# Dealing eight SBUF slots in fixed rotation to loads and outgoing images of a Winograd-style convolution

## The chip, the cores and the metric

The kernel runs on one core of one Trainium2 chip. The metric is the time of one execution in microseconds of the device, the median of several runs. A run's *span*, from its first instruction to the end of its work, is about 1.8 us shorter than its time. Some executions are slower than the others of the same kernel; a run counts as *slow* when it is over 1.5% above the fastest run of the same kernel, and else as *fast*.

## The reference

```python
batch, c_in, h, w, c_out = 16, 64, 64, 64, 128      # x: fp32; weight: 128 x 64 x 3 x 3, fp32
x_pad = pad(x, one pixel of zeros around each image)
output[b, co] += weight[co, ci, kh, kw] * x_pad[b, ci, kh:kh+h, kw:kw+w]     # all b, co, ci, kh, kw
```

It is a 3x3 convolution. The input is 16.8 MB of fp32, the output 33.5 MB of fp32.

## The kernel before

Two images form a *pair*, so that 2 x 64 input channels fill 128 partitions; there are eight pairs. The kernel combines rows so that two output rows share one product (`G1` with row sums `ss`). TensorE makes the products in PSUM (the memory that it accumulates in), ScalarE (ACT) copies the shared one to `ut`, and VectorE (DVE) adds that to each of the others, which writes the output images `ot`. GpSimd (POOL) makes the row sums.

Memory is what this study is about: SBUF, the core's on-chip memory of 128 partitions. One fp32 pair (`xf`) takes 16 KB of each partition, and so does one outgoing image (`ot`); a pair has two of these. All come from one pool of eight 16 KB slots:

```python
big = ctx.enter_context(tc.tile_pool(name="big", bufs=8))
NH = 5
cuts = [(0, 18), (18, 34), (34, 50), (50, 64)]

def load(p):                                   # pairs 0 to 4: fp32, cast to fp16 by ScalarE later
    xf[p] = big.tile([128, H, W], F32, tag="big", name="xf")
    for lo, hi in cuts if p == 0 else [(0, H)]:
        keep(nc.sync.dma_start(xf[p][:, lo:hi, :], x_rows[128*p : 128*p+128, lo:hi, :]))

def outs(p):                                   # the two outgoing images of a pair
    ots[p] = [big.tile([128, H // 2, 2, W], F32, tag="big", name="ot") for _ in range(2)]

def load_cast(p):                              # pairs 5 to 7: the DMA casts to fp16, other memory
    xs[p] = xpool.tile([128, H, W], F16, tag="xc", name="xc")
    keep(nc.gpsimd.dma_start(xs[p], x_rows[128*p : 128*p+128, :, :]))

for p in range(NH): load(p)
outs(0)
# ... weights ...
for p in range(NP):                            # NP = 8
    if p not in ots: outs(p)
    # POOL: row sums of pair p+1; at p == 0 also load_cast(5..7)
    for blk in range(4):
        U = group([(G1, None)]);  us = [scalar.copy(U[b2]) for b2 in 0, 1]
        # ScalarE: some casts xf -> xs of coming pairs
        A = group([(G21, 1), (G0, -1)])
        # VectorE: ot row 0 of each row pair = A + us   (L184)
        Bt = group([(G01, 0), (G2, 2)])
        # VectorE: ot row 1 = Bt + us                   (L187)
        parts = {3: (0, 64)} if p < NP - 1 else {1: (0, 32), 3: (32, 64)}
        if blk in parts:                       # 2 MB per image; the last pair in two halves
            lo, hi = parts[blk]
            for b2 in range(2):
                keep(nc.sync.dma_start(out_rows[2*p + b2, :, lo:hi, :], ots[p][b2] ...))   # L192
```

A new tile in a used slot has to wait until the slot's last user is done: for a load, that its casts and row sums were made; for an outgoing image, that its store has landed. With `bufs=8` and one tag, the framework chooses the slot. The waits in the program as built tell its choice: pair 2's first image got load 1's slot, and its *second image got the slot of store 0's first image*. Pairs 3 to 5 are mixed in the same way: one image in a load's slot, the other in that of an earlier store.

## Time and profile before

| | before |
|---|---|
| time, median of 3 (range) | 133.56 us (133.37 to 134.36) |
| span of the profiled run | 132.2 us |
| TensorE busy | 108.4 us (82%) |
| longest wait of VectorE | 9.1 us, for an outgoing DMA |
| arithmetic ends / last store lands | 122.6 us / 131.0 us |

The profile's page cuts the span into 40 slices of 3.3 us; a digit is the busy share in tenths, and `PEclk` is the granted TensorE clock:

```profile
span 132.2 us, 2428 instructions
...
PE   0389999999992059999999999999999999997000
...
PEclk9999999999999757999999999999999999999965
DMA  4999999999999999999999999699469937999992
GB/s 138 304 376 451 416 451 402 352 315 310 327 310 327 315 322 330 404 441 412 451 416 421 441 412 426 288 397 471 169 273 441 397 164 317 456 414 394 434 436 89
```

TensorE has one hole, near 40 to 48 us. DMA is full until then and long after, and has holes, stretches in which the engines run out of transfers, only after 82 us (6, 4, 6, 3, 7). The list of waits (engine and tile, what it waited for, total us, times, longest) names the hole:

```profile
DVE ot L184 <- DMA out_dram<-ot: 9.1, 1, 9.1
PE acc L164 <- DVE ot L184: 7.3, 1, 7.3
```

One event, told twice: VectorE waits once for 9.1 us, and TensorE, whose PSUM tiles are not emptied meanwhile, stands still for 7.3 us. The timeline of VectorE shows where (start, length, engine, line, what; in brackets the idle time before it and what ended it):

```profile
37.20 0.69 DVE L184 TENSOR_TENSOR ot<-acc,ut 128x512 f32<-128x512 f32 x1 [0.72 <-PE acc L164]
46.99 0.69 DVE L184 TENSOR_TENSOR ot<-acc,ut 128x512 f32<-128x512 f32 x1 [9.10 <-DMA out_dram<-ot]
```

These are the first adds of pair 2's two images. The second starts at 46.99 us, just after store 0's first image landed (46.86 us, issued at 23.10: it stood in line behind loads that were still coming). The chain of waits, followed back from the last instruction, runs through that store:

```profile
PE 63%; DMA 22%; DVE 3%; ACT 2%; issue 1%; DVEq 1%; SPq 0%
PE acc L164 63%; DMA out_dram<-ot 18%; DMA xf<-in_x_dram 4%; DVE ot L184 2%; ACT xs L62 1%; DVE ot L187 1%; DVE ss L89 1%; DVEq L221 0%; ACT ut L178 0%; SPq L45 0%; DVEq L184 0%
```

By stretches (length, busy time of each engine, granted clock, mean share of the 16 DMA engines that was busy, where 1 or a little over is full, GB/s), TensorE is the limit late in the kernel, with DMA not far behind:

```profile
core 0: us, PE busy (x) PEld busy (x) DVE busy (x) ACT busy (x) POOL busy (x), PEclk, DMA share, GB/s
45.00:51.00 6.00, 3.27 (x16) 1.35 (x17) 4.00 (x7) 0.00 (x0) 0.00 (x0) 0.50 1.04 328
84.00:96.00 12.00, 12.00 (x116) 6.10 (x114) 9.21 (x16) 3.81 (x8) 0.82 (x1) 1.00 0.83 351
96.00:108.00 12.00, 12.00 (x116) 6.08 (x112) 9.21 (x16) 4.29 (x8) 0.00 (x0) 1.00 0.83 351
```

The first of these lines shows an echo of the hole: after the standstill the granted clock was 0.50. The Trainium skill, "TensorE: Matmul & The Clock Gate", section "What's actually happening", says that an idle TensorE falls to half its clock after some 3.4 us and is released by activity; this trace agrees (idle from 40.4 us, half clock from 44.6 to 51.4 us).

### The profile page before, as it was taken

What the parts mean: (1) busy time and instruction counts of PE and PEld (TensorE: products, weight loads), DVE (VectorE), ACT (ScalarE), POOL (GpSimd) and SP (SyncE); (2) the same over time, 40 slices, a digit from 0 to 9 for tenths busy, and PEclk for the clock granted to TensorE, in tenths of its full rate; (3) what the DMA queues carried; (4) which work ended last, traced back from release to release, by engine and by line L of the source; (5) the groups of instructions that cost most, each with busy time, mean ns of one, the idle gap of its engine ahead of it and who ended that gap; (6) DMA issues with size and microseconds to landing.
All of it is one profiled execution on the core that took longest, in us unless ns stands there. A gap on an engine that the chain in (4) does not pass through costs nothing.

```text
span 132.2 us, 2428 instructions
## 1 busy us (share of the span) xinstructions
PE 108.4 (82%) x978; PEld 55.3 (42%) x978; DVE 84.1 (64%) x135; ACT 55.9 (42%) x88; POOL 33.8 (26%) x23
## 2 busy tenths in 40 slices
PE   0389999999992059999999999999999999997000
PEld 0335455555550024455545455545554555443000
DVE  0278857877720075787777877877787778777000
ACT  3283878969694004843333333333333333332000
POOL 2000399967076000390047006600000000000000
PEclk9999999999999757999999999999999999999965
DMA  4999999999999999999999999699469937999992
GB/s 138 304 376 451 416 451 402 352 315 310 327 310 327 315 322 330 404 441 412 451 416 421 441 412 426 288 397 471 169 273 441 397 164 317 456 414 394 434 436 89
DMA packets 4330, 47.62 MB, mean 360 GB/s; under 512 B 480, under 2 KB 480, under 8 KB 1120
## 3 DMA queue, kind: packets, MB, share of 16 engines
q1 hardware_dynamic: 3888, 44.34, 80.4%
q0 software_dynamic: 432, 3.15, 11.4%
q8 instruction: 7, 0.11, 0.3%
q14 instruction: 3, 0.02, 0.0%
HBM read 17.07 MB, written 33.55 MB: 383 GB/s over the span
## 4 chain that ended last, share of the span: by engine, by line
PE 63%; DMA 22%; DVE 3%; ACT 2%; issue 1%; DVEq 1%; SPq 0%
PE acc L164 63%; DMA out_dram<-ot 18%; DMA xf<-in_x_dram 4%; DVE ot L184 2%; ACT xs L62 1%; DVE ot L187 1%; DVE ss L89 1%; DVEq L221 0%; ACT ut L178 0%; SPq L45 0%; DVEq L184 0%
## 5 line engine op out<-in xcount | busy, mean ns | idle before, releaser
L164 PEld LDWEIGHTS <-Wt 64*128 64x128 f16 x960 | 54.1, 96 | 61.6 <-issue 13.5
L164 PE MATMUL acc<-xs,Wt 64*128 64x504 f16 (+3 forms) x480 | 63.2, 385 | 7.4 <-DVE ot L184 7.3
L184 DVE TENSOR_TENSOR ot<-acc,ut 128x512 f32<-128x512 f32 x64 | 41.3, 685 | 31.4 <-PE acc L164 19.9
L178 ACT COPY ut<-acc 128x512 f32<-128x512 f32 x64 | 34.4, 590 | 59.0 <-issue 44.1
L187 DVE TENSOR_TENSOR ot<-acc,ut 128x512 f32<-128x512 f32 x64 | 41.1, 684 | 0.0
L164 PE MATMUL acc<-ss,Wt 64*128 64x504 f16 (+1 forms) x192 | 36.1, 392 | 1.5 <-DVE ss L89 1.5
L164 PE MATMUL acc<-xc,Wt 64*128 64x504 f16 (+3 forms) x288 | 35.0, 373 | 0.0
L89 POOL TENSOR_TENSOR ss<-xf 128x1024 f16<-128x1024 f32 x8 | 18.8, 2369 | 20.1 <-DMA xf<-in_x_dram 14.0
L62 ACT CAST xs<-xf 128x1024 f16<-128x1024 f32 (+2 forms) x20 | 20.4, 1058 | 0.9 <-DMA xf<-in_x_dram 0.9
L89 POOL TENSOR_TENSOR ss<-xc 128x1024 f16<-128x1024 f16 x6 | 12.6, 2128 | 30.3 <-issue 30.3
L89 DVE TENSOR_TENSOR ss<-xf 128x512 f16<-128x512 f32 x4 | 2.8, 689 | 3.4 <-DMA xf<-in_x_dram 3.4
L107 PE MATMUL wp<-ident,w 128*64 128x128 f16 x18 | 1.3, 328 | 4.1 <-DVE w L79 4.1
L107 PEld LDWEIGHTS <-w 128*64 128x64 f16 x18 | 1.1, 210 | 4.1 <-DVE w L79 4.1
L79 DVE CAST w<-w_raw 128x576 f16<-128x576 f32 x1 | 0.5, 460 | 3.6 <-DMA w_raw<-in_weight_dram 3.6
L71 POOL DMA_DIRECT2D xc<-in_x_dram x3 | 1.8, 599 | 0.0
L109 ACT CAST Wt<-wp 128x384 f16<-128x384 f32 x1 | 0.5, 479 | 2.8 <-PE wp L107 2.8
L109 ACT ACT_TABLE_LOAD x1 | 1.3, 1283 | 0.7 <-PEq L210 0.7
L114 ACT CAST Wt<-wp 128x384 f16<-128x384 f32 x1 | 0.5, 479 | 0.5 <-DVE Wt L112 0.5
L111 DVE TENSOR_TENSOR Wt<-wp,Wt 128x384 f16<-128x384 f32 x1 | 0.5, 549 | 0.0
L112 DVE TENSOR_TENSOR Wt<-wp,Wt 128x384 f16<-128x384 f32 x1 | 0.5, 546 | 0.0
L115 ACT CAST Wt<-wp 128x384 f16<-128x384 f32 x1 | 0.5, 484 | 0.0
masks.py:199 POOL TENSOR_SCALAR_AFFINE_SELECT ident<-ident 128x128 f16<-128x128 f16 x1 | 0.3, 294 | 0.1
(5 smaller groups left out, 0.6 us busy)
## 6 DMA issues: line engine op xcount, KB each, us to landing
out_dram<-ot SPq DMA_DIRECT2D x14, 2048.0 KB, 11.8
xf<-in_x_dram SPq DMA_DIRECT2D x4, 2048.0 KB, 19.7
out_dram<-ot SPq DMA_DIRECT2D x4, 1024.0 KB, 8.3
xc<-in_x_dram POOLq DMA_DIRECT2D x3, 1024.0 KB, 24.4
xf<-in_x_dram SPq DMA_DIRECT2D x2, 512.0 KB, 6.2
xf<-in_x_dram SPq DMA_DIRECT2D x1, 576.0 KB, 5.0
xf<-in_x_dram SPq DMA_DIRECT2D x1, 448.0 KB, 7.8
w_raw<-in_weight_dram SPq DMA_DIRECT2D x1, 288.0 KB, 2.9
```

Source lines behind the costliest of these rows:

```text
L62: keep(nc.scalar.copy(xs[p][:, lo:hi, :], xf[p][:, lo:hi, :]))
L71: keep(nc.gpsimd.dma_start(xs[p], x_rows[128 * p : 128 * p + 128, :, :]))
L79: keep(nc.vector.tensor_copy(w16, w_raw))
L89: eng.tensor_add(ss[p][:, lo : lo + n, :], v[:, lo : lo + n, 0, :], v[:, lo : lo + n, 1, :])
L107: nc.tensor.matmul(wp[q : q + 64, k * CO : k * CO + CO], w16[:, t::9], ident)
L109: keep(nc.scalar.copy(wrow(G1), wps[1]))
L111: keep(nc.vector.tensor_sub(wrow(G21), wps[2], wrow(G1)))
L112: keep(nc.vector.tensor_sub(wrow(G01), wps[0], wrow(G1)))
L164: nc.tensor.matmul(tiles[b2][:, lo - j0 : hi - j0, c_lo:c_hi], Wt[p0 : p0 + 64, wi, kw, :], rhs, start=i == 0, stop=i == n - 1,)
L178: keep(nc.scalar.copy(ut, U[b2]))
L184: nc.vector.tensor_add(ots[p][b2][:, j0 : j0 + RB, 0, :], A[b2], us[b2])
L187: nc.vector.tensor_add(ots[p][b2][:, j0 : j0 + RB, 1, :], Bt[b2], us[b2])
```

## The change

The intent is that a tile takes the slot whose last user began longest ago, so that no outgoing image waits for a store that was only just issued. Eight tags with one buffer each fix the choice by hand:

```diff
-    big = ctx.enter_context(tc.tile_pool(name="big", bufs=8))
+    big = ctx.enter_context(tc.tile_pool(name="big", bufs=1))
 ...
+    slot = [0]
+
+    def next_slot(shape, name):
+        slot[0] += 1
+        return big.tile(shape, F32, tag=f"slot{(slot[0] - 1) % 8}", name=name)
 ...
-        xf[p] = big.tile([128, H, W], F32, tag="big", name="xf")
+        xf[p] = next_slot([128, H, W], "xf")
 ...
-        ots[p] = [big.tile([128, H // 2, 2, W], F32, tag="big", name="ot") for _ in range(2)]
+        ots[p] = [next_slot([128, H // 2, 2, W], "ot") for _ in range(2)]
```

Loads 0 to 4 take slots 0 to 4, pair 0 takes 5 and 6, pair 1 takes 7 and 0, pair 2 takes 1 and 2 (loads 1 and 2), pair 3 takes 3 and 4, and from pair 4 on each pair takes the slots of the pair four before it. No instruction and no size changes.

## The prediction

> **What bounds the kernel now.** The span is 132.2 us (median run 133.56). The list of waits shows two long ones of one event: the vector engine's first add of an image pair waits 9.1 us for an outgoing DMA, and the tensor engine 7.3 us for that add. In the timeline it is pair 2: its first such add ends its wait at 46.99, when pair 0's first store (issued 23.10) landed. The chain of waits runs through that store (18%), then 72 us of unbroken matmuls; from 48 to 120 us TensorE is busy throughout. The second limit is close: DMA is busy 92% of the span, without a hole to about 82 us, at some 428 GB/s; later holes sum to 7.5 us (its packets, in 3 us stretches).
>
> **What the change does.** No instruction, size or order changes; only addresses, and so waits. In the program as built before, pair 2's images took load 1's slot and that of *store 0's first image*; pairs 3 to 5 mix likewise. With rotation, pair 2 takes loads 1 and 2, pair 3 loads 3 and 4, pair 4 pair 0's slots, 5 pair 1's, 6 pair 2's, 7 pair 3's.
>
> **Costed.**
> - Pair 2's second image needs load 2's casts (ended 31.3) and Pool sums (26.4), against its turn near 37.9: no wait. The 9.1 us goes; pair 3 starts near 50.0, not 59.16 (pairs start 12.8 us apart).
> - Pair 3 needs load 4's casts (expected near 47.5) and Pool sums (41.9): little or no wait.
> - Pair 4, near 62.8, needs store 0 (landed 55.5); pair 5, near 75.6, store 1 (65.25); pairs 6 and 7, at 88 and 101, stores 2 and 3 (about 75 and 85): no wait.
> - So arithmetic ends near 113.4, not 122.6: 9.1 us earlier.
> - The stores cannot follow. After store 1 lands at 65.25, ten 2 MB stores at 4.85 us (their landings in the full stretch) and four of 1 MB at 2.43 us remain: 65.25 + 48.5 + 9.7 = 123.5 us. A pair's stores are issued every 12.8 us and take 9.7, so the backlog shrinks but just does not empty before the end. Last landing 123.5, not 131.0: 7.5 us gained, the same as the sum of the holes.
>
> The Trainium skill, "DMA: Bandwidth & Descriptors", section "Where 436 GB/s comes from", gives 435 GB/s as the ceiling at the SBUF ports; this trace's 428 agrees, so I expect no faster stores.
>
> **On the critical path:** 7.5 of the 9.1 us. The end turns from compute-bound to store-bound.
>
> **Predicted: 126.1 us, 8 in 10 within 125.0 to 127.8.** Faster by over 2%: 0.96; within 2%: 0.035; slower: 0.005.
>
> **What the profile would show.** Right: the 9.1 and 7.3 us waits gone; no gap of TensorE over 1 us after 7 us; no dip of its clock between 43 and 53 us; last add near 113.4; DMA at 9 in every slice to the end; the last store landing some 10 us after its issue (8.4 before), the chain ending in outgoing DMAs. Wrong in part: a new vector-engine wait at pair 3 (for casts or sums) or from pair 4 on (for stores); DMA holes after 82 us.
>
> **What would make it wrong.** ScalarE has six casts in pair 2 and may be late for pair 3's second image. Without the pause the throttle may take back clock. The store rate may differ with a deeper backlog: 1% is 0.6 us. If DMA holes stay, the time is 127 or more.

## The result, and the profile after

A ratio is the mean time of one kernel's fast runs over that of the other's fast runs of the same rounds, so it is not quite the ratio of the medians quoted.

| | before | after |
|---|---|---|
| time, median of 4 runs (range) | 133.96 us (133.37 to 134.66) | 127.97 us (127.81 to 128.02) |
| ratio, 95% interval | | 0.9549 (0.9494 to 0.9604) |
| span of the profiled run | 132.2 us | 126.2 us |
| arithmetic ends | 122.6 us | 113.5 us |
| last store lands | 130.98 us | 124.98 us |

The change saves 6 us, 4.5%. The predicted time was 126.1 us, and 127.97 lies 0.17 us above its range.

The same lines of the page after:

```profile
span 126.2 us, 2428 instructions
...
PE   0479999999999999999999999999999999950000
...
PEclk9999999999999999999999999999999999996555
DMA  4999999999999999999999999999999999999970
GB/s 121 298 434 431 426 426 436 343 317 317 288 332 332 312 309 306 369 447 447 410 415 421 436 452 426 415 415 426 452 436 415 421 415 462 423 395 434 423 301 10
```

TensorE's hole and the dip of its clock are gone, and so are DMA's holes. But look at the end: arithmetic stops four slices before the span does, and DMA's last slices are not full: 7, then 0, with 301 and 10 GB/s. In the list of waits, no entry of VectorE or TensorE for an outgoing DMA is left. VectorE's timeline at pairs 2 and 3:

```profile
37.30 1.30 DVE L190 TENSOR_TENSOR ot<-acc,ut 128x512 f32<-128x512 f32 x2 [0.69 <-PE acc L170]
...
50.11 1.29 DVE L190 TENSOR_TENSOR ot<-acc,ut 128x512 f32<-128x512 f32 x2 [0.69 <-PE acc L170]
```

Both images of pair 2 are now added to in one go, and pair 3 starts at 50.11 us instead of 59.16. By stretches:

```profile
45.00:51.00 6.00, 6.00 (x60) 3.06 (x58) 4.58 (x8) 3.32 (x6) 4.20 (x2) 1.00 1.03 321
84.00:96.00 12.00, 12.00 (x116) 6.09 (x114) 9.24 (x16) 4.30 (x8) 0.00 (x0) 1.00 1.01 431
96.00:108.00 12.00, 12.00 (x116) 6.08 (x114) 9.24 (x16) 4.30 (x8) 0.00 (x0) 1.00 1.02 433
```

DMA is now as full as TensorE. The chain of waits has a trap:

```profile
PE 82%; DMA 4%; DVE 2%; issue 1%; DVEq 0%; SPq 0%
PE acc L170 82%; DMA xf<-in_x_dram 4%; DVE ot L190 1%; DVE ss L95 1%; DVE ot L193 0%; DVEq L227 0%; SPq L51 0%; DVEq L190 0%
```

It reads as if TensorE bound the whole kernel. But the shares sum to only about 90%: the chain starts from the last *instruction*, VectorE's add that ends at 113.45 us, and of the 12.7 us after that, 11.5 pass until the last store lands. Stores are not instructions. They show in the time from issue to landing of the stores, first before, then after:

```profile
DMA to landing us min/median/max: 6.3/10.9/31.8
```

```profile
DMA to landing us min/median/max: 9.7/17.6/31.2
```

**Where 1.5 us of the expected gain went.** The trace records when each of the 16 DMA engines reports its share of a store done. Worked out from these records, in us from the start (not a view of the profile):

```
store                     before: issued fastest slowest spread   after: issued fastest slowest spread
pair 1, second image              36.50   63.18   65.25   2.07            36.63   63.17   65.15   1.98
pair 3, second image              71.39   82.59   84.90   2.30            62.25   82.59   84.61   2.02
pair 4, first image               83.59   89.72   89.95   0.23            74.46   87.50   89.59   2.09
pair 6, second image             109.81  120.18  121.30   1.12           100.67  111.79  115.20   3.41
pair 7, last half                122.61  129.97  130.98   1.00           113.47  121.57  124.98   3.42
```

The *fastest* engine keeps the pace that was predicted: from 63.17 to 111.79 us it does ten stores, 4.86 us each (predicted 4.85), and the four halves take 9.78 us (predicted 9.7). But a store has landed only when its *slowest* engine is done. Before, the first hole in the queue (near 83 us) let all engines start the next store together, and the spread fell from 2.30 to 0.23 us. After, no hole comes, and the spread grows to 3.42 us. The Trainium skill, "DMA: Bandwidth & Descriptors", section "Why a DMA increments its semaphore by 16 and not by 1", says that a DMA runs on up to 16 engines that finish independently; these records agree, and give the size.

In both traces, between 54 us and the end of the arithmetic, some 16 KB store packets take 630 to 680 ns where the others take 611. They follow each other end to end, as packets of a single engine do, and after the change there are nine or ten of them in every 6 us, as many as one engine can do in that time. So one engine seems to have all of them. They cost it about 0.35 us in every 6 us, which is 0.28 us a store. The spread fits that: it stays between 1.98 and 2.24 us up to the store that landed at 89.59 us, and from there, where the slowed engine would have become the last one, it grows by 0.3 us a store until the arithmetic nears its end.

A second thing holds single engines up. The profile's page, before and after, lists a queue of instruction packets (packets, MB, share of 16 engines):

```profile
q8 instruction: 7, 0.11, 0.3%
```

Each is 16 KB. After the change, four of the seven came between 59 and 101 us; each took an engine 0.88 to 0.97 us, and the store packet that follows it end to end took 0.98 to 1.02 us instead of 0.61. That engine is then 1.3 us behind.

### The profile page after: what moved, and what is told of

Its sections match the earlier page's. It is cut to its first block, busy times and chain, and to the rows that moved or that the text cites. A ratio compares the mean times of both kernels' runs of the same rounds, so it can differ in the third digit from the quotient of the medians.

```text
span 126.2 us, 2428 instructions
## 1 busy us (share of the span) xinstructions
PE 106.4 (84%) x978; PEld 53.6 (42%) x978; DVE 84.4 (67%) x135; ACT 55.9 (44%) x88; POOL 33.8 (27%) x23
## 4 chain that ended last, share of the span: by engine, by line
PE 82%; DMA 4%; DVE 2%; issue 1%; DVEq 0%; SPq 0%
PE acc L170 82%; DMA xf<-in_x_dram 4%; DVE ot L190 1%; DVE ss L95 1%; DVE ot L193 0%; DVEq L227 0%; SPq L51 0%; DVEq L190 0%
## 5 line engine op out<-in xcount | busy, mean ns | idle before, releaser
L170 PEld LDWEIGHTS <-Wt 64*128 64x128 f16 x960 | 52.5, 96 | 53.8 <-issue 4.1
L170 PE MATMUL acc<-xs,Wt 64*128 64x504 f16 (+2 forms) x480 | 56.5, 383 | 0.0
L170 PE MATMUL acc<-xc,Wt 64*128 64x504 f16 (+3 forms) x288 | 32.7, 373 | 0.0
L170 PE MATMUL acc<-ss,Wt 64*128 64x504 f16 (+1 forms) x192 | 27.0, 384 | 1.5 <-DVE ss L95 1.5
```

The source lines that it names most:

```text
L170: nc.tensor.matmul(tiles[b2][:, lo - j0 : hi - j0, c_lo:c_hi], Wt[p0 : p0 + 64, wi, kw, :], rhs, start=i == 0, stop=i == n - 1,)
```

## The experiments

Two questions: is the one wait the whole cause of the gain, and why did 1.5 us of it go missing? For the second, *theory A* says that the stores bind and that the slowest of 16 drifting engines sets the end; *theory B* that a deep backlog slows all engines alike; a third view is that arithmetic still binds the end.

### One slot exchanged

```diff
+    swapped = {10: 5, 13: 2}
     def next_slot(shape, name):
+        n = swapped.get(slot[0], slot[0] % 8)
         slot[0] += 1
-        return big.tile(shape, F32, tag=f"slot{(slot[0] - 1) % 8}", name=name)
+        return big.tile(shape, F32, tag=f"slot{n}", name=name)
```

> The rotation, but with two slots exchanged: pair 2's second image takes store 0's first slot again, as before the change, and pair 4's first image takes load 2's. Theory (one wait explains it all): the 9.1 us wait of the vector engine for the first store is back, the tensor engine idles 7.3 us, span 132.2 us, time within 1% of before. Rival (the mixing of pairs 3 to 5 mattered as well): the time lies clearly between, 129 to 132 us.

Measured: 134.75 us, ratio to before 1.0087 (1.0032 to 1.0142), span 132.2 us. Its list of waits:

```profile
DVE ot L193 <- DMA out_dram<-ot: 10.0, 1, 10.0
PE acc L173 <- DVE ot L193: 8.2, 1, 8.2
```

This slot choice alone brings the whole time back, with pairs 3 to 7 free of such waits in either kernel. The theory holds. The wait is 0.9 us longer than before because arithmetic reached pair 2 that much sooner in this run, while the store landed at nearly the same time (46.95 us, 46.86 before).

### Less arithmetic

A wrong result. From pair 3 on, one of three column taps is left out.

```diff
-                n = 3 * len(wi_rows)
+                kws = (1, 0, 2) if p < 3 else (1, 0)
+                n = len(kws) * len(wi_rows)
 ...
-                    for kw in (1, 0, 2):
+                    for kw in kws:
```

> A wrong result on purpose: from pair 3 on every block leaves out one of three column taps, so the tensor engine has a third less to do and arithmetic ends some 8 us earlier (near 105 us). Theory (the end is bound by the stores): the fastest DMA engine's last landing stays at 121.6 us and the time within 1% of the changed kernel's 127.97 us. Rival (arithmetic still bounds the end): time falls by over 5 us.

Measured: 127.07 us (126.97 to 127.52), ratio to before 0.9536. Arithmetic ended at 97.5 us, 16 us earlier than in the changed kernel (more than the 8 us expected), and only 0.9 us of that shows in the time. The fastest engine's last landing was 121.60 us (121.57 in the changed kernel). The stores bind, not the arithmetic. What moved is the spread: 2.39 us instead of 3.42. The slow packets stopped near 95 us, when TensorE did (95.05 us).

```profile
96.00:108.00 12.00, 0.00 (x0) 0.00 (x0) 1.52 (x3) 0.00 (x0) 0.00 (x0) 0.56 1.00 430
108.00:120.00 12.00, 0.00 (x0) 0.00 (x0) 0.00 (x0) 0.00 (x0) 0.00 (x0) 0.50 1.00 425
```

Those two stretches are the plainest picture of the bound: no engine computes, and DMA is full at the same rate.

### A store on fifteen engines

```diff
                 for b2 in range(2):
+                    for p0, p1 in [(0, 120), (120, 128)] if (p, b2) == (6, 1) else [(0, 128)]:
-                    keep(nc.sync.dma_start(out_rows[2 * p + b2, :, lo:hi, :], ...[:, lo:hi, :]))
+                        keep(nc.sync.dma_start(out_rows[2 * p + b2, p0:p1, lo:hi, :], ...[p0:p1, lo:hi, :]))
```

The Trainium skill, "DMA: Bandwidth & Descriptors", again in the section "Why a DMA increments its semaphore by 16 and not by 1", says that a DMA issued like these uses the largest number of engines up to 16 that divides the slowest dimension of both its sides, the lowest-numbered ones, and that the unused engines' share of the semaphore is counted at once. So 120 partitions should leave one engine out.

> Pair 6's second store is issued as 120 partitions (15 DMA engines, 8 partitions each) and 8 partitions (8 engines, one each); bytes are the same, one engine gets 4.9 us less and eight get 0.6 us more. Theory A (the 1.5 us missing is one DMA engine that lags the others by 2 us and finishes the last store alone): if the laggard is the engine left out, the spread of the last landing falls from 3.4 to 2.1-2.7 us and the time by 0.7 to 1.3 us, to about 127; if it is one of the eight, the time rises by 0.6; otherwise no change. Theory B (all engines store more slowly under a deep backlog): no change to plus 0.3 us, and an even spread.

Measured: 132.79 us (130.92 to 134.86), ratio to before 0.988; three of the six runs count as slow, the profiled one too. This is a miss; even its fast runs (130.92 to 132.31) are about 3 us above the changed kernel. In the profiled run, one of 16 completions came at once, 0.95 us after the issue, and the next 10.5 us later, as that section says. But some thirty of the 16 KB packets then took 1.1 to 1.5 us instead of 0.61, between 108 and 120 us, and a few longer still. Which engine lags could therefore not be told, and why the packets doubled is open; the slow profile may have a part in it. The run still bears on theory A, by making an uneven store on purpose: the fastest engine's last landing was 122.25 us, little later than in the changed kernel, while the slowest came 9.45 us after it.

### All stores in halves

```diff
-            parts = {3: (0, 64)} if p < NP - 1 else {1: (0, 32), 3: (32, 64)}
+            parts = {1: (0, 32), 3: (32, 64)}
```

> Every pair's store is cut in two halves of 32 rows, issued after blocks 1 and 3; bytes are the same, packets are 8 KB instead of 16 KB. In the trace one engine's 16 KB packets took 644 to 670 ns instead of 611 from 54 us on, while the 8 KB packets of pair 7 took 309 ns on all. Theory A1 (that engine lags because of these long packets): the slow packets vanish, the spread at the last landing falls from 3.4 to about 2 us; 8 KB packets cost 0.03 us more per store, so the time falls by about 1 us to 127. Theory A2 (the engine is slowed as long as the arithmetic runs, whatever the packet): slow 8 KB packets appear and the spread stays over 3 us, time 128 to 128.5.

Measured: 129.14 us (128.74 to 129.34), ratio to before 0.9678: about 1 us slower than the changed kernel. A1 falls and A2 stands, though the time is 0.6 us above A2's range too. Slow 8 KB packets (over 322 ns instead of 309) cost 0.65 to 0.71 us in every 12 us until 102 us, and none was seen after 112 us (TensorE ended at 111.8); the spread at the end was 3.84 us. The packets of pair 7 are fast in the changed kernel because most of them go out after the arithmetic has ended, not because they are small. The smaller packets cost a little as well: the fastest engine ended at 122.02 us, 0.45 us later.

### The changed kernel again

> The changed kernel once more, to have it beside the others of this call: 127.8 to 128.1 us, the last store landing in the profile near 125.0 with its fastest DMA engine near 121.6.

Measured: 128.20 us (128.09 to 128.43), ratio 0.9578; fastest engine 121.73 us, spread 3.57 us, last landing 125.30 us. This is 0.3 us over what was expected and the yardstick for the three runs below, which ran on the same chip.

### The first load in two pieces

```diff
-        for lo, hi in cuts if p == 0 else [(0, H)]:
+        for lo, hi in [(0, 32), (32, H)] if p == 0 else [(0, H)]:
```

> The first load in two pieces of 32 rows (8 KB packets) instead of four (3.6 to 4.6 KB packets). From the durations in the trace its packets should keep the 16 DMA engines 4.9 us instead of 5.7. Arithmetic starts about 1 us later. Theory (the kernel is bound by DMA from the first load to the last store, arithmetic has 5 us to spare): every later landing is about 0.7 us sooner, time 127.3. Rival (arithmetic is still on the chain, as the profile's chain of waits says): time rises by about 1 us, to 129.

Measured: 127.62 us (127.56 to 128.33), ratio to before 0.9546, correct; 0.6 us less than the changed kernel on the same chip by the medians, near the 0.7 expected. The next load (pair 1's) landed in all its engines by 13.55 us, against 15.20 in the yardstick, and in its fastest engine 0.54 us sooner. At the end the fastest engine was 0.31 us sooner (121.42 us) and the spread 0.32 us smaller (3.25 us); the second part was not foreseen and may be chance. Arithmetic did not start later; it ended 1.1 us *sooner* than in the yardstick, which was not expected. Five of the six runs lie under every run of the yardstick, the sixth among them. The direction follows theory A, but because arithmetic was not delayed, the run does not test the rival as sharply as meant. It is the fastest correct version found, but the gain over the yardstick, 0.5%, is small and the intervals of the two ratios overlap.

### Less DMA

A wrong result: pair 7's load is left out.

```diff
-            for q in range(NH, NP):
+            for q in range(NH, NP - 1):
                 load_cast(q)
+            xs[NP - 1] = xs[NP - 2]
```

> A wrong result on purpose: pair 7's load is left out and pair 6's is used twice; arithmetic is unchanged. Theory (store-bound, engines drift while no hole lets them fall in step): the queue now runs empty before pair 7's last stores, the spread of the last landing falls under 1.2 us, the last landing is near 120.2 us instead of 125.0 and the time near 123.2. Rival (arithmetic bounds the end): last landing and time unchanged within 0.5 us.

Measured: 123.88 us (123.59 to 124.67), 4.3 us under the yardstick. Arithmetic had the same amount to do (it ended at 112.1 us, 1.4 us sooner). DMA's holes are back:

```profile
DMA  4999999999999999999999999999999859999991
```

(This span is 121.8 us, so slices are shorter; the hole is near 98 us.) With it the engines fell in step: the spread fell from 3.53 us at pair 5's last store to 0.82 us at the next, and was 1.06 us at the end. The last landing was 120.61 us (expected 120.2). That is theory A's prediction, and against "arithmetic binds": arithmetic ended only 1.4 us sooner, and could not have given more than that.

### One tap of three

A wrong result: the edit of "Less arithmetic" with `(1,)` instead of `(1, 0)`.

> A wrong result on purpose: from pair 3 on one of three column taps alone, so that the tensor engine issues about half as many instructions a microsecond as before while the vector engine is busy throughout. In the changed kernel one DMA engine loses about 0.32 us in every 6 us to packets of 644 ns and more while the arithmetic runs. If what slows it goes with the tensor engine's instructions, the loss falls to about 0.15 us in 6 us; if with the vector and scalar engines' work, it stays at 0.3 or more. In both cases the loss stops when the arithmetic ends, and the fastest engine's last landing stays at 121.6 us, time 126.3 to 127.2.

Measured: 126.22 us (126.13 to 126.46). Between 60 and 84 us TensorE issued 8.4 weight loads and matmuls a microsecond, against 18.7 in the changed kernel and 16.7 in "Less arithmetic"; VectorE was busy all the time:

```profile
60.00:84.00 24.00, 21.13 (x103) 6.31 (x101) 24.00 (x41) 11.61 (x20) 4.20 (x2) 0.93 1.01 429
```

Here the threshold matters. Counted from 636 ns on, the slow packets cost 0.07 to 0.10 us in 6 us. But in this run the slowed packets are nearly as many as before and only less slow: most take 625 to 636 ns, and a count from 636 ns misses them. Counted from 625 ns on in every run, the loss between 60 and 84 us is 0.22 us in 6 us, against 0.35 in the changed kernel and 0.35 in "Less arithmetic". So what slows them goes with TensorE's work, not with the work of VectorE or ScalarE, which had more to do in each microsecond here: 45% of TensorE's instructions left some 60% of the loss. Whether it is the instructions or the data that they read is not told apart, as both fell together. The fastest engine ended at 121.16 us and the spread was 2.32 us.

## Why the prediction was right or wrong

**Right.** The two waits of 9.1 and 7.3 us vanish, TensorE has no later gap over 1 us, and its clock does not dip. No new wait took their place: pair 3, 4, 5, 6 and 7 started at 50.11, 62.80, 75.61, 88.42 and 101.22 us, against 50.0, 62.8, 75.6, 88 and 101 as predicted, and the last add ended at 113.45 (113.4 predicted). The last store landed 11.5 us after its issue (some 10 predicted). The fear that ScalarE's casts come late was unfounded (they ended at 47.52 us). DMA has no hole left, and the end turned from compute-bound to store-bound: 16 us less arithmetic saved 0.9 us, and one load less saved 4.3 us.

**Wrong: the size of one term.** The failing step is "65.25 + 48.5 + 9.7 = 123.5 us". It measured the pace of a store from *landings*, that is from the slowest engine, in a stretch where the spread happened to stay near 2 us, and went on as if 16 engines were one. The runs show three parts: the fastest engine's pace, which was right to 0.2 us over 14 stores (so theory B falls); the starting point, which was 0.1 us early; and the spread, which grew from 1.98 to 3.42 us, 1.44 us. Together 1.5 us, so the last landing is 124.98. The check "the same as the sum of the holes" misled: busy time summed over the engines is conserved, but the mean engine does not end the kernel. On average the engines ended 1.12 us after the fastest (0.16 before), so the mean engine did gain 7.4 us, from 130.13 to 122.69; the slowest, which ended 3.42 us after the fastest (1.00 before), gained 6.0. The remaining 0.4 us of the error in time is a mismatch of runs: the landings came from a profiled run of 133.95 us, but the 7.5 us were taken off the median of 133.56.

So the gain was 9.1 us in arithmetic, of which 6 us reached the end. The prediction put 1.6 us of loss on the stores' backlog; 1.5 us more went to the drift of the DMA engines.

**Also wrong.** The chain of waits does not end in outgoing DMAs: it cannot, as it starts from an instruction.

**Shown and not shown.** That a hole brings the engines in step is shown by three traces (before, the one slot exchanged, and "Less DMA") and by the lack of it in all traces without a hole. That part of the spread comes from what TensorE's work does to single engines is shown by two runs that took some of that work away and left the fastest engine within 0.6 us of where it was. These runs had fewer instruction packets too (6 and 4 against 7), so they do not tell this from the slowed packets; that the slowed packets set the last 1.3 us of growth rests on their rate, 0.28 us a store against 0.3. Why packets slow while TensorE works is open; so are whether recording the trace itself has a part in it, and which engine it is. That it is always one and the same engine is inferred from packets that follow each other end to end, and from their number.

## What to carry to other kernels

When a slot is shared by loads and stores, look at what its last user *waits for*: a store that stands behind loads in the queue frees its slot late, and a fixed rotation that hands out the oldest slot can save the whole wait. Before counting such a wait as gain, add up the second limit to the end: here DMA was 92% busy and took back a third. And where a DMA queue never runs empty, reckon the end from the slowest of its engines, not from bytes over bandwidth. Among the stores that landed after 59 us (the uneven one aside) no spread fell by more than 0.25 us until a hole came; it grew while TensorE worked at full rate, and in "One tap of three" it stayed (2.31 us at 60 us, 2.32 at the end).

## What the Trainium skill lacked or had wrong

- "DMA: Bandwidth & Descriptors" says that the engines of a DMA finish independently and, in its section on the iDMA fabric, that a bulk load runs at the pace of its slowest engine. It does not say that engines that drifted apart stay so while the queue never runs empty, nor how far they drift: here from 1.98 to 3.42 us over ten 2 MB stores, while one hole cut the spread from 2.30 to 0.23 us.
- No page that I read tells that store packets slow with TensorE's work: one engine lost about 0.35 us in 6 us at 17 to 19 weight loads and matmuls a microsecond, 0.22 us at 8.4, nothing once TensorE had ended. Nor what an instruction packet of 16 KB costs the engine that carries it: 1.3 us here.
- The first page's rule for how many engines a store uses does not say what an uneven store costs: after a 120-partition store on 15 engines and one of 8 partitions, some thirty 16 KB packets took 1.1 to 1.5 us instead of 0.61 (one trace, of a slow run).
- In the same page, section "Where 436 GB/s comes from", the sentence that the HBM side (about 358 GB/s) binds transfers between HBM and SBUF misleads when read alone, though the page itself goes on to a single-core measurement near 425 GB/s: with one core running, the full stretches here, from 60 to 108 us after the change, moved 425 to 433 GB/s. "HBM Reference", section "Specifications (TRN2)", has it right (about 425 GB/s for a core that streams alone).
